# An up projection turned round: activations stationary and a DRAM bounce in place of weights stationary, in a float32 decoder layer

## The chip, the cores and the metric

The kernel runs on one core of a Trainium2 chip. The metric is the device time of one execution in microseconds (us), lower is better. Besides the timed runs there is one execution recorded by the hardware profiler; all rows below come from it. The engines are PE (TensorE, matmul), DVE (VectorE), ACT (ScalarE), POOL (GpSimd) and SP (SyncE, which here issues nearly all DMAs).

## The reference, cut to what matters

One decoder layer on 256 tokens of width 2048: two attention mixers, gates and an output projection, then a squared-ReLU MLP of inner width 8192. The change is in the MLP:

```python
h2 = rms_norm(x, g_mlp)
x = x + jnp.square(jax.nn.relu(h2 @ w_up)) @ w_down      # w_up 2048 x 8192, w_down 8192 x 2048
```

All tensors are float32. The kernel keeps nearly float32 accuracy by splitting each operand into a rounded part *hi* and a rest *lo* and summing three products, hi·hi, hi·lo and lo·hi.

## The kernel before, in words

**Slots.** The whole weight traffic is cut into *slots*. A slot is a weight tile of two 128-row k-blocks by 512 columns. A 1 MB DMA (L127, issued by SP) brings the weights of two slots into a tile `raw` (3 buffers). For each slot `split` makes `hi` on ACT (L138, a cast) and `lo` on DVE (L139, a subtraction); these have 3 buffers each, and a new one can be written once PE has finished with the one three slots back. The main loop is written out by hand: in turn `j` it emits `split(j + 2)`, the DMA of a later piece if one is due, what tables `at_dma[j]` and `at_post[j]` hold, and then the matmuls of slot `j`. So each engine gets its instructions in the order of the turns, and waits in that order.

**Chunks.** Eight slots (k = 2048) make a chunk of 512 output columns. All projections but the up projection go through `tok_chunk`: the activations, transposed and split (`xT`, `yT`, `mT`, `h`, each [128, k-block, hi/lo, 256 tokens]), are the stationary operand, and the split weights the moving one. Two banks of PSUM hold 2 x 128 tokens by 512 columns. Per slot this is `tok_major`: for two token halves and two k-blocks

```python
nc.tensor.matmul(o, lhsT=s_hi, rhs=hi[:, kk, a:b], ...)   # L164
nc.tensor.matmul(o, lhsT=s_hi, rhs=lo[:, kk, a:b], ...)   # L165
nc.tensor.matmul(o, lhsT=s_lo, rhs=hi[:, kk, a:b], ...)   # L166
```

that is 12 matmuls of 512 columns per slot. **The up projection** (`up_chunk`, 8 chunks in each of two halves `hf`) has the operands the other way round: the weights are stationary and `x1T` is moving (L540 hi weight x [hi, lo] tokens, 512 columns; L542 lo weight x hi tokens, 256 columns). Its output comes out feature-major in four PSUM banks, which is the layout that the down projection wants, and `post` (L554 to L563) adds the two halves of a bank, squares the ReLU and splits the result into `h0` or `h1` in three turns after the chunk.

**The bounce.** Where a token-major result must become a stationary operand, `bounce_chunk` turns it. DVE transposes it in 32 x 32 blocks (L198) into `tq`; SP writes `tq` to a DRAM tile `scr` with four DMAs (L203, 128 KB each) and reads it back with one (L208, 512 KB, tile `st`); ACT and DVE then write the hi and lo parts (`split_tr`, L145 and L146, four each). With the chunk's last slot called e, the caller passes j = e + 2, and

```python
on(at_post, j, blk)             # turn e+2: DVE transposes
on(at_dma, j + 1, wr)           # turn e+3: SP writes scr
on(at_dma, j + steps[0], rd)    # steps = (3, 6): turn e+5: SP reads st
on(at_post, j + steps[1], p)    # turn e+8: ACT and DVE unpack
```

`tq` and `st` have one buffer, `scr` two, `tmp` tiles (`u`, `ma`, `mb`) five. The bounce is used before for the queries and keys, for the mixed branches (`mix_b`, default steps) and for the output projection (`out_done`, where the second chunk has steps (5, 9)).

**Order of the stages**: input projection (23 chunks, with attention among the later ones), the branches, the output projection, up and down of half 0, up and down of half 1. The first two chunks of the output projection and of the up projection of half 0 are interleaved by `in_pairs` (first 6 slots of one, 6 of the other, then 2 and 2), since their last k-blocks arrive late. `j_up` is the first slot of the up projection.

Of the kernel before, what the change touches and what calls it, by code (L numbers as in the profile page):

```python
# [9 lines left out]
F32 = mybir.dt.float32  # L10
F32R = mybir.dt.float32r
AF = mybir.ActivationFunctionType
ALU = mybir.AluOpType
AX = mybir.AxisListType

P = 128
S = 256
# [15 lines left out]
CW = 512  # L33
WARM = (10, 7)
EARLY = (1, 2, 3, 4, 5, 6)
KD = D // P
# [30 lines left out]
def hybrid_block_kernel(ctx: ExitStack, tc: tile.TileContext, x, g_mix, w_in, q_norm_a, k_norm_a,  # L67
                        q_norm_b, k_norm_b, rel_bias, w_branch_a, w_branch_b, w_out, g_mlp, w_up,
                        w_down, hot, mask, out):
    nc = tc.nc  # L70
# [13 lines left out]
    def bank(tag="fill"):  # L84
        return ps.tile([P, CW], F32, name=tag, tag=tag)

    def tmp(name="tmp"):
        return tp.tile([P, CW], F32, name=name, tag="tmp")

    at_fill, at_post, at_dma = {}, {}, {}  # L90

    def on(table, j, fn):
        table.setdefault(j, []).append(fn)
# [18 lines left out]
    def stream(src, k0, nk, c0, main, pieces=None):  # L112

        for a in pieces or range(0, nk, 4):
            ap = src[k0 + a * P:k0 + (a + 4) * P, c0:c0 + CW].rearrange("(k p) c -> p k c", p=P)
            for b in (0, 2):
                slots.append((ap, b, a + b, main))
# [24 lines left out]
    def split_tr(dst_hi, dst_lo, src, gain=None):  # L142

        if gain is None:
            nc.scalar.copy(dst_hi, src)  # L145
            nc.vector.tensor_tensor(dst_lo, src, dst_hi.bitcast(F32), op=ALU.subtract)  # L146
        else:
            nc.scalar.activation(dst_hi, src, AF.Copy, scale=gain)
            nc.vector.scalar_tensor_tensor(dst_lo, src, gain, dst_hi.bitcast(F32), op0=ALU.mult,
                                           op1=ALU.subtract)  # L150

    def tok_major(banks, actT, k, first, last, hi, lo, between=None):


        parts = [(0, 0, CW), (1, 0, CW)] if len(banks) == 2 else [(0, 0, CW), (1, 0, S), (1, S, CW)]
        order = [(i, kk) for i in range(len(parts)) for kk in range(2)]
        if between:
            order = [(i, kk) for kk in range(2) for i in range(2)]
        for i, (n, kk) in enumerate(order):
            t, a, b = parts[n]  # L160
            o = banks[n][:, 0:b - a]
            s_hi = actT[:, k + kk, 0, t * P:(t + 1) * P]
            s_lo = actT[:, k + kk, 1, t * P:(t + 1) * P]
            nc.tensor.matmul(o, lhsT=s_hi, rhs=hi[:, kk, a:b], start=first and kk == 0, stop=False)  # L164
            nc.tensor.matmul(o, lhsT=s_hi, rhs=lo[:, kk, a:b], start=False, stop=False)  # L165
            nc.tensor.matmul(o, lhsT=s_lo, rhs=hi[:, kk, a:b], start=False, stop=last and kk == 1)  # L166
            if between and i == 1:
                between()

    def tok_chunk(src, k0, nk, c0, actT, ka, done):  # L170

        st = {}

        def main(j, k, hi, lo):
            if k == 0:
                st["b"] = [bank("acc") for _ in range(2)]
            tok_major(st["b"], actT(), ka + k, k == 0, k + 2 == nk, hi, lo, T.get("mid") if j == 0 else None)
            if k + 2 == nk:
                done(st["b"], j)

        return lambda *p: stream(src, k0, nk, c0, main, p)
# [11 lines left out]
    T = {}  # L193


    def blocks(dst, src):

        nc.vector.transpose(dst.rearrange("p j n r -> p n j r"), src.rearrange("p n (j m) -> p n j m", m=32))  # L198

    def scatter(scr, src):  # L200

        for i in range(4):
            nc.sync.dma_start(out=scr[:, :, :, i].rearrange("t j m f -> m (t j) f"),  # L203
                              in_=src[32 * i:32 * i + 32].rearrange("m t j f -> m (t j) f"))

    def gather(dst, scr):

        nc.sync.dma_start(out=dst, in_=scr.rearrange("t j m i f -> (j m) t (i f)"))  # L208
# [100 lines left out]
    def v_done(br, c):  # L309
        def done(banks, j):  # L310
            def p():
                for t in range(2):
                    o = T["v" + br][:, t, c * CW:(c + 1) * CW]
                    if t:
                        nc.vector.tensor_scalar(o, banks[t], rstd[:, t:t + 1], None, op0=ALU.mult)
                    else:
                        nc.scalar.activation(o, banks[t], AF.Copy, scale=rstd[:, t:t + 1])
            on(at_post, j + 1, p)
        return done
# [141 lines left out]
    def bounce_chunk(src, dst, c, j, gain, steps=(3, 6)):  # L461

        st = {}

        def blk():
            st["tq"] = tq = ap_.tile([P, 2, 4, CW // 4], F32, name="tq")
            for t in range(2):
                blocks(tq[:, t].rearrange("p j (n r) -> p j n r", r=32),
                       src()[t].rearrange("p (n d) -> p n d", d=P))

        def wr():
            st["scr"] = dp.tile([2, 4, 32, 4, CW // 4], F32, name="scr", bufs=2)
            scatter(st["scr"], st["tq"])

        def rd():
            st["st"] = ap_.tile([P, 2, CW], F32, name="st")
            gather(st["st"], st["scr"])

        def p():
            v = st["st"].rearrange("p t (i n r) -> p n t i r", i=4, r=32)  # L480
            for k in range(4):
                hi, lo = (dst()[:, 4 * c + k, a].rearrange("p (t i r) -> p t i r", t=2, i=4) for a in range(2))
                split_tr(hi, lo, v[:, k], None if gain is None else gT[:, gain + 4 * c + k:gain + 4 * c + k + 1])

        on(at_post, j, blk)
        on(at_dma, j + 1, wr)
        on(at_dma, j + steps[0], rd)
        on(at_post, j + steps[1], p)
# [38 lines left out]

    def up_chunk(hf, g):

        st = {}  # L530
        name = f"h{g // 4}"

        def main(j, k, hi, lo):
            if k == 0:
                st["b"] = [bank("fill" if (g + hf) % 2 else "acc") for _ in range(4)]
            for n in range(4):
                b = st["b"][n]
                for kk in range(2):
                    xk = T["x1T"][:, k + kk]
                    nc.tensor.matmul(b, lhsT=hi[:, kk, n * P:(n + 1) * P], rhs=xk.rearrange("p a q -> p (a q)"),  # L540
                                     start=(k + kk == 0), stop=False)
                    nc.tensor.matmul(b[:, S:], lhsT=lo[:, kk, n * P:(n + 1) * P], rhs=xk[:, 0],  # L542
                                     start=False, stop=(k + kk == KD - 1))
            if k + 2 == KD:
                for i in range(3):
                    on(at_post, j + 1 + i, lambda i=i: post(i))

        def post(i):

            if i < 2:  # L550
                for n in (2 * i, 2 * i + 1):
                    u = tmp("u")
                    st[n] = u
                    nc.scalar.copy(u[:, 0:S], st["b"][n][:, S:])  # L554
                for n in (2 * i, 2 * i + 1):
                    u = st[n]
                    nc.vector.tensor_tensor(u[:, S:], st["b"][n][:, 0:S], u[:, 0:S], op=ALU.add)
                    nc.vector.scalar_tensor_tensor(u[:, 0:S], u[:, S:], 0.0, u[:, S:], op0=ALU.max, op1=ALU.mult)
            if i > 0:
                for n in (2 * i - 2, 2 * i - 1):  # L560
                    h = T[name][:, (g % 4) * 4 + n]
                    nc.scalar.copy(h[:, 0], st[n][:, 0:S])
                    nc.vector.tensor_tensor(h[:, 1], st[n][:, 0:S], h[:, 0].bitcast(F32), op=ALU.subtract)  # L563

        return lambda *p: stream(w_up, 0, KD, (hf * 8 + g) * CW, main, p)

    def down_chunk(hf, c):
        st = {}
# [26 lines left out]
    for c in range(23):  # L595
        if c < 6:
            done = qk_done("aq" if c < 3 else "ak", 4 * c)
        elif c < 9:
            done = v_done("a", c - 6)
        elif c < 13:  # L600
            done = qk_done("bq" if c < 11 else "bk", 4 * (c - 9))
        elif c < 15:
            done = v_done("b", c - 13)
        else:
            done = gate_done(c - 15)
# [9 lines left out]
    for hf in range(2):  # L615
        j_half.append(len(slots))
        ups = [up_chunk(hf, g) for g in range(8)]
        if hf:
            for f in ups:
                f()  # L620
        else:
            in_pairs(ups)
        for c in range(4):
            down_chunk(hf, c)
# [8 lines left out]
    for br, nh, tag in (("a", NA, "T0"), ("b", NB, "T2")):  # L633
        t = big.tile([P, 3 * nh * S], F32, name="qkv" + br, tag=tag)
# [57 lines left out]
    for i in range(2, 8):  # L692
        st = {}
# [38 lines left out]
    n = len(slots)  # L732
    done_split, done_load = 2, 3
    for j in range(n + 1):
# [13 lines left out]
        if j < n:  # L748
            hi, lo = split_t.pop(j)
# [38 lines left out]
```

## Time and profile before

| | us |
|---|---|
| median of 3 timed runs | 1409.17 (1408.72 to 1409.3) |
| the profiled execution | 1408.98 |
| its span (first to last instruction) | 1406.9 |
| PE busy | 1401.6 |
| DVE busy | 811.2 |
| ACT busy | 650.2 |
| granted PE clock | 1.00 of full speed (2.4 GHz) throughout |

Busy times are shares of one span and overlap. Matmuls are pipelined, so a busy PE says that matmuls were in flight, not how many columns a second went through; the distance from one matmul's start to the next says that.

### The profile page before, as it was taken

What the parts mean: (1) busy time and instruction counts of PE and PEld (TensorE: products, weight loads), DVE (VectorE), ACT (ScalarE), POOL (GpSimd) and SP (SyncE); (2) the same over time, 40 slices, a digit from 0 to 9 for tenths busy, and PEclk for the clock granted to TensorE, in tenths of its full rate; (3) what the DMA queues carried; (4) which work ended last, traced back from release to release, by engine and by line L of the source; (5) the groups of instructions that cost most, each with busy time, mean ns of one, the idle gap of its engine ahead of it and who ended that gap; (6) DMA issues with size and microseconds to landing.
All of it is one profiled execution on the core that took longest, in us unless ns stands there. A gap on an engine that the chain in (4) does not pass through costs nothing.

```text
span 1406.9 us, 17199 instructions
## 1 busy us (share of the span) xinstructions
PE 1401.6 (100%) x6773; PEld 1179.3 (84%) x6773; DVE 811.2 (58%) x989; ACT 650.2 (46%) x956; POOL 28.6 (2%) x44
## 2 busy tenths in 40 slices
PE   9999999999999999999999999999999999999998
PEld 7888888888888888888888888888888888888888
DVE  5556546676555545766656666444445656554443
ACT  7554445554444464445545445333334444443332
POOL 1101000010000000000000000000000000000000
PEclk9999999999999999999999999999999999999999
DMA  8777986778566655888766655656566566656662
GB/s 284 230 240 230 284 276 220 242 255 279 183 222 210 219 183 181 261 279 276 245 203 192 188 180 182 206 182 203 184 199 190 180 184 188 195 182 215 203 208 91
DMA packets 171128, 300.95 MB, mean 214 GB/s; under 512 B 6936, under 2 KB 37032, under 8 KB 171048
## 3 DMA queue, kind: packets, MB, share of 16 engines
q1 hardware_dynamic: 170856, 299.84, 66.1%
q8 instruction: 53, 0.87, 0.3%
q14 instruction: 27, 0.22, 0.0%
q0 software_dynamic: 160, 0.01, 0.0%
q10 hardware_dynamic: 32, 0.01, 0.0%
HBM read 280.43 MB, written 19.40 MB: 213 GB/s over the span
## 4 chain that ended last, share of the span: by engine, by line
PE 99%; DMA 0%; DVE 0%; issue 0%
PE acc L164 20%; PE acc L165 20%; PE acc L166 20%; PE fill L540 9%; PE acc L540 9%; PE acc L542 4%; PE fill L542 4%; PE fill L164 4%; PE fill L165 4%; PE fill L166 4%; PE fill L383 1%; PE fill L430 1%; PE fill L382 0%; PE fill L432 0%; PE fill L220 0%; DMA x<-in_x_dram 0%
## 5 line engine op out<-in xcount | busy, mean ns | idle before, releaser
L139 DVE TENSOR_TENSOR lo<-raw,hi 128x1024 fp32r<-128x1024 f32 (+1 forms) x498 | 606.3, 1219 | 573.7 <-ACT hi L138 572.3
L138 ACT CAST hi<-raw 128x1024 fp32r<-128x1024 f32 (+1 forms) x498 | 522.3, 1049 | 701.1 <-PE acc L166 422.0
L164 PE MATMUL acc<-hi,xT 128*128 128x512 f32 x736 | 289.4, 393 | 0.0
L165 PE MATMUL acc<-lo,xT 128*128 128x512 f32 x736 | 286.7, 390 | 0.0
L166 PE MATMUL acc<-hi,xT 128*128 128x512 f32 x736 | 286.6, 389 | 0.0
L540 PE MATMUL acc<-x1T,hi 128*128 128x512 f32 x512 | 181.3, 399 | 0.0
L540 PE MATMUL fill<-x1T,hi 128*128 128x512 f32 x512 | 181.3, 399 | 0.0
L166 PEld LDWEIGHTS acc<-hi,xT 128*128 128x128 f32 x736 | 138.2, 188 | 29.0
L164 PEld LDWEIGHTS acc<-hi,xT 128*128 128x128 f32 x736 | 138.4, 188 | 28.8 <-issue 0.6
L165 PEld LDWEIGHTS acc<-lo,xT 128*128 128x128 f32 x736 | 138.3, 188 | 28.6 <-DVE lo L139 0.4
L542 PE MATMUL acc<-x1T,lo 128*128 128x256 f32 x512 | 143.8, 281 | 0.0
L542 PE MATMUL fill<-x1T,lo 128*128 128x256 f32 x512 | 143.8, 281 | 0.0
L540 PEld LDWEIGHTS acc<-x1T,hi 128*128 128x128 f32 x512 | 96.2, 188 | 24.1
L540 PEld LDWEIGHTS fill<-x1T,hi 128*128 128x128 f32 x512 | 96.2, 188 | 24.1
L164 PE MATMUL acc<-hi,h 128*128 128x512 f32 (+1 forms) x288 | 108.7, 377 | 0.0
L166 PE MATMUL acc<-hi,h 128*128 128x512 f32 (+1 forms) x288 | 108.7, 377 | 0.0
L165 PE MATMUL acc<-lo,h 128*128 128x512 f32 (+1 forms) x288 | 108.6, 377 | 0.0
L542 PEld LDWEIGHTS fill<-x1T,lo 128*128 128x128 f32 x512 | 96.7, 189 | 0.0
L542 PEld LDWEIGHTS acc<-x1T,lo 128*128 128x128 f32 x512 | 96.7, 189 | 0.0
L165 PE MATMUL fill<-lo,h 128*128 128x512 f32 (+1 forms) x256 | 96.4, 376 | 0.0
L164 PE MATMUL fill<-hi,h 128*128 128x512 f32 (+1 forms) x256 | 96.3, 376 | 0.0
L166 PE MATMUL fill<-hi,h 128*128 128x512 f32 (+1 forms) x256 | 96.2, 376 | 0.0
(123 smaller groups left out, 1199.9 us busy)
## 6 DMA issues: line engine op xcount, KB each, us to landing
raw<-in_w_in_dram SPq DMA_DIRECT2D x89, 1024.0 KB, 5.7
raw<-in_w_up_dram SPq DMA_DIRECT2D x64, 1024.0 KB, 5.3
raw<-in_w_down_dram SPq DMA_DIRECT2D x64, 1024.0 KB, 5.3
raw<-in_w_out_dram SPq DMA_DIRECT2D x16, 1024.0 KB, 5.4
scr<-tq SPq DMA_DIRECT2D x72, 128.0 KB, 5.5
raw<-in_w_branch_b_dram SPq DMA_DIRECT2D x8, 1024.0 KB, 5.7
st<-scr SPq DMA_DIRECT2D x13, 512.0 KB, 5.6
raw<-in_w_branch_a_dram SPq DMA_DIRECT2D x4, 1024.0 KB, 5.4
```

The lines of the kernel that those rows point to most:

```text
L138: nc.scalar.copy(hi[:, o], t[:, o])
L139: nc.vector.tensor_tensor(lo[:, o], t[:, o], hi[:, o].bitcast(F32), op=ALU.subtract)
L164: nc.tensor.matmul(o, lhsT=s_hi, rhs=hi[:, kk, a:b], start=first and kk == 0, stop=False)
L165: nc.tensor.matmul(o, lhsT=s_hi, rhs=lo[:, kk, a:b], start=False, stop=False)
L166: nc.tensor.matmul(o, lhsT=s_lo, rhs=hi[:, kk, a:b], start=False, stop=last and kk == 1)
L383: nc.tensor.matmul(b[:, P:P + S], lhsT=q[:, 1], rhs=k, start=True, stop=True)
L430: nc.tensor.matmul(st["o"][:, o:o + S], lhsT=v[:, 0, h * HD:(h + 1) * HD], rhs=pt[:, 0:2], start=(g == 0 or not joint), stop=False)
L540: nc.tensor.matmul(b, lhsT=hi[:, kk, n * P:(n + 1) * P], rhs=xk.rearrange("p a q -> p (a q)"), start=(k + kk == 0), stop=False)
L542: nc.tensor.matmul(b[:, S:], lhsT=lo[:, kk, n * P:(n + 1) * P], rhs=xk[:, 0], start=False, stop=(k + kk == KD - 1))
```

## The change

The up projection becomes a `tok_chunk` like the others: `x1T` is stationary, the split weights move, and two banks hold the result token-major. After the chunk ACT takes the ReLU from PSUM into a `tmp` tile, DVE multiplies it with the bank once more (a square of the ReLU), and `bounce_chunk` with the default steps transposes it through DRAM into `h0` or `h1`. The order of chunks, `in_pairs` for half 0 and the down projection stay as they are.

```diff
     def up_chunk(hf, g):
-        def main(j, k, hi, lo):
-            if k == 0:
-                st["b"] = [bank("fill" if (g + hf) % 2 else "acc") for _ in range(4)]
-            for n in range(4):
-                b = st["b"][n]
-                for kk in range(2):
-                    xk = T["x1T"][:, k + kk]
-                    nc.tensor.matmul(b, lhsT=hi[:, kk, n * P:(n + 1) * P], rhs=xk.rearrange("p a q -> p (a q)"),
-                                     start=(k + kk == 0), stop=False)
-                    nc.tensor.matmul(b[:, S:], lhsT=lo[:, kk, n * P:(n + 1) * P], rhs=xk[:, 0],
-                                     start=False, stop=(k + kk == KD - 1))
...
-        def post(i):
...
-        return lambda *p: stream(w_up, 0, KD, (hf * 8 + g) * CW, main, p)
+        def done(banks, j):
+            hs = []
+
+            def p():
+                for t in range(2):
+                    u = tmp("u")
+                    nc.scalar.activation(u, banks[t], AF.Relu)
+                    nc.vector.tensor_tensor(u, banks[t], u, op=ALU.mult)
+                    hs.append(u)
+            on(at_post, j + 1, p)
+            bounce_chunk(lambda: hs, lambda: T[f"h{g // 4}"], g % 4, j + 2, None)
+        return tok_chunk(w_up, 0, KD, (hf * 8 + g) * CW, lambda: T["x1T"], 0, done)
```

In the order of PE's instructions, the first slot of the up projection (slot `j_up`) reads before as follows; `acc_5348` to `acc_5351` are the four banks, `hi_5304` and `lo_5305` the slot's weights, and "..." stands where the second k-block repeats the two rows.

```order
L540 MATMUL acc_5348<-x1T_4690,hi_5304 128x512
L542 MATMUL acc_5348<-x1T_4690,lo_5305 128x256
...
L540 MATMUL acc_5349<-x1T_4690,hi_5304 128x512
L542 MATMUL acc_5349<-x1T_4690,lo_5305 128x256
...
L540 MATMUL acc_5350<-x1T_4690,hi_5304 128x512
L542 MATMUL acc_5350<-x1T_4690,lo_5305 128x256
...
L540 MATMUL acc_5351<-x1T_4690,hi_5304 128x512
L542 MATMUL acc_5351<-x1T_4690,lo_5305 128x256
```

The same slot of the changed kernel, on PE:

```order
L164 MATMUL acc_5348<-hi_5304,x1T_4690 128x512
L165 MATMUL acc_5348<-lo_5305,x1T_4690 128x512
L166 MATMUL acc_5348<-hi_5304,x1T_4690 128x512
...
L164 MATMUL acc_5349<-hi_5304,x1T_4690 128x512
L165 MATMUL acc_5349<-lo_5305,x1T_4690 128x512
L166 MATMUL acc_5349<-hi_5304,x1T_4690 128x512
```

Sixteen matmuls (8 of 512 and 8 of 256 columns) became twelve of 512; the slot streams 6144 columns both times.

SP's queue behind the interleaved pair of half 0 held only weight loads before. In the changed kernel it stands as follows; the pair's first chunk writes `scr_5665` and reads `st_5715`, its second `scr_5717` and `st_5756`.

```order
L203 DMA scr_5665<-tq_5646 32x8x128 x4
L127 DMA raw_5694<-in_w_up_dram 128x4x512
L208 DMA st_5715<-scr_5665 128x2x512
L203 DMA scr_5717<-tq_5696 32x8x128 x4
L127 DMA raw_5738<-in_w_up_dram 128x4x512
L208 DMA st_5756<-scr_5717 128x2x512
L127 DMA raw_5774<-in_w_up_dram 128x4x512
L127 DMA raw_5816<-in_w_up_dram 128x4x512
```

Two bounces of five DMAs each now stand among the weight loads, and the read into `st_5756` stands ahead of the load of `raw_5774`; `st_5715` and `st_5756` are the same single buffer.

ACT's queue at the same place in the changed kernel (turns `j_up + 21` to `j_up + 25`): the casts of weights (`hi`) and the unpacking of the two bounces into `h0`.

```order
L138 CAST hi_5770<-raw_5644 128x1024
L145 CAST h0_5368<-st_5715 128x256 x4
L138 CAST hi_5796<-raw_5694 128x1024
L138 CAST hi_5812<-raw_5694 128x1024
L145 CAST h0_5368<-st_5756 128x256 x4
L138 CAST hi_5838<-raw_5738 128x1024
L536 ACTIVATE u_5842<-acc_5676 128x512
L536 ACTIVATE u_5845<-acc_5677 128x512
L138 CAST hi_5862<-raw_5738 128x1024
```

The unpacking of the second bounce stands two casts behind that of the first, and the casts of the following slots stand behind it.

## Rows read from the trace of the kernel before

**Rows 1.** The page: the span, the busy time of the engines with its share and number of instructions, and the chain of work that ended last by engine.

```profile
span 1406.9 us, 17199 instructions
PE 1401.6 (100%) x6773; PEld 1179.3 (84%) x6773; DVE 811.2 (58%) x989; ACT 650.2 (46%) x956; POOL 28.6 (2%) x44
PE 99%; DMA 0%; DVE 0%; issue 0%
```

**Rows 2.** Busy time by stretch: up of half 0, down of half 0, up of half 1, down of half 1. Columns: stretch, its length, busy time of PE, of the weight loads on PE, of DVE, ACT and POOL (instructions in brackets), granted clock, share of the DMA engines, GB/s.

```profile
691.20:872.10 180.90, 180.90 (x1025) 156.82 (x1024) 113.96 (x163) 88.16 (x132) 0.00 (x0) 1.00 0.62 192
872.10:1046.20 174.10, 174.10 (x770) 144.19 (x769) 86.66 (x82) 69.83 (x72) 0.00 (x0) 1.00 0.59 193
1046.20:1227.10 180.90, 180.90 (x1025) 156.76 (x1025) 109.78 (x150) 83.35 (x120) 0.00 (x0) 1.00 0.60 186
1227.10:1402.90 175.80, 175.80 (x866) 149.11 (x864) 85.42 (x82) 67.69 (x70) 0.00 (x0) 1.00 0.56 183
```

**Rows 3.** PE in order of time (start, duration, instruction) at the end of the output projection and the start of the up projection. Starts are to be compared; the durations overlap.

```profile
690.76 0.39 PE L165 MATMUL acc<-lo,mT 128*128 128x512 f32 x1
690.99 0.39 PE L166 MATMUL acc<-hi,mT 128*128 128x512 f32 x1
691.22 0.39 PE L540 MATMUL acc<-x1T,hi 128*128 128x512 f32 x1
691.44 0.28 PE L542 MATMUL acc<-x1T,lo 128*128 128x256 f32 x1
691.56 0.40 PE L540 MATMUL acc<-x1T,hi 128*128 128x512 f32 x1
691.79 0.28 PE L542 MATMUL acc<-x1T,lo 128*128 128x256 f32 x1
691.91 0.40 PE L540 MATMUL acc<-x1T,hi 128*128 128x512 f32 x1
```

**Rows 4.** Groups of instructions by line and shape over the whole span (count, busy us, mean ns of one, idle time before): the first five are those that the change removes outside PE, the others are operations of the same shape as those it adds.

```profile
L554 ACT COPY u<-acc 128x256 f32<-128x256 f32 x32 | 10.2, 370 | 0.0
L562 ACT CAST h<-u 128x256 fp32r<-128x256 f32 x64 | 23.1, 409 | 1.2 <-DVE u L558 1.2
L557 DVE TENSOR_TENSOR u<-acc,u 128x256 f32<-128x256 f32 x32 | 13.4, 418 | 0.0
L558 DVE SCALAR_TENSOR_TENSOR u<-u 128x256 f32<-128x256 f32 x64 | 27.2, 425 | 2.2
L563 DVE TENSOR_TENSOR h<-u,h 128x256 fp32r<-128x256 f32 x64 | 24.1, 418 | 0.0
L333 ACT ACTIVATE G<-acc,rstd 128x512 f32<-128x512 f32 x6 | 4.1, 679 | 0.0
L497 DVE TENSOR_TENSOR mb<-acc,G 128x512 f32<-128x512 f32 x8 | 5.5, 684 | 0.0
```

**Rows 5.** DVE, ACT and SP in order of time around a bounce of `mix_b` (start, duration of the run, instruction, count, and in brackets the idle time before it and what ended it).

```profile
561.40 1.30 DVE L198 STREAM_TRANSPOSE tq<-ma 128x512 f32<-128x512 f32 x2
562.73 2.06 SPq L203 DMA_DIRECT2D scr<-tq  x4
568.83 0.38 SPq L208 DMA_DIRECT2D st<-scr  x1
574.42 1.05 ACT L138 CAST hi<-raw 128x1024 fp32r<-128x1024 f32 x1 [1.67 <-PE acc L166]
575.38 1.32 ACT L145 CAST mT<-st 128x256 fp32r<-128x256 f32 x4
577.72 1.43 DVE L146 TENSOR_TENSOR mT<-st,mT 128x256 fp32r<-128x256 f32 x4
```

**Rows 6.** An ordinary slot of the output projection, whose first matmul started at 604.14: PE's first matmul, and a cast and a subtraction 13 slots on.

```profile
604.14 0.39 PE L164 MATMUL acc<-hi,mT 128*128 128x512 f32 x1
639.70 1.05 ACT L138 CAST hi<-raw 128x1024 fp32r<-128x1024 f32 x1 [1.67 <-PE acc L166]
640.79 1.23 DVE L139 TENSOR_TENSOR lo<-raw,hi 128x1024 fp32r<-128x1024 f32 x1 [1.50 <-ACT hi L138]
```

**Rows 7.** DMAs by line: size of one and median us from issue to landing; then the least, median and greatest landing time of the reads into `st`.

```profile
raw<-in_w_up_dram SPq DMA_DIRECT2D x64, 1024.0 KB, 5.3
scr<-tq SPq DMA_DIRECT2D x72, 128.0 KB, 5.5
st<-scr SPq DMA_DIRECT2D x13, 512.0 KB, 5.6
DMA to landing us min/median/max: 3.9/5.6/6.9
```

**Rows 8.** Who waited for whom from 520 to 690 us (branches and output projection, with seven bounces), longest first in total: total us, times, longest.

```profile
ACT hi L138 <- PE acc L166: 83.5, 55, 1.7
DVE lo L139 <- ACT hi L138: 59.1, 42, 1.8
ACT junk L514 <- DVE x L512: 6.7, 3, 2.9
DVE tq L198 <- DMA scr<-tq: 0.8, 1, 0.8
ACT hi L138 <- ACT hi L138: 0.5, 2, 0.3
```

**Rows 9.** Busy time by stretch, with the columns of rows 2: a stretch of the input projection, and one that begins 4 us before the output projection and covers its first 36 us.

```profile
160.00:200.00 40.00, 40.00 (x178) 33.11 (x178) 19.69 (x17) 16.22 (x17) 0.00 (x0) 1.00 0.88 283
600.00:640.00 40.00, 40.00 (x178) 33.11 (x178) 24.59 (x30) 17.52 (x23) 0.00 (x0) 1.00 0.86 294
```

More of the change, by code (lines that the diff above doesn't have):

```diff
@@ L528, in up_chunk @@
     def up_chunk(hf, g):
-        st = {}
-        name = f"h{g // 4}"
-        def main(j, k, hi, lo):
-            if k == 0:
-                st["b"] = [bank("fill" if (g + hf) % 2 else "acc") for _ in range(4)]
-            for n in range(4):
-                b = st["b"][n]
-                for kk in range(2):
-                    xk = T["x1T"][:, k + kk]
-                    nc.tensor.matmul(b, lhsT=hi[:, kk, n * P:(n + 1) * P], rhs=xk.rearrange("p a q -> p (a q)"),
-                                     start=(k + kk == 0), stop=False)
-                    nc.tensor.matmul(b[:, S:], lhsT=lo[:, kk, n * P:(n + 1) * P], rhs=xk[:, 0],
-                                     start=False, stop=(k + kk == KD - 1))
-            if k + 2 == KD:
-                for i in range(3):
-                    on(at_post, j + 1 + i, lambda i=i: post(i))
-        def post(i):
-            if i < 2:
-                for n in (2 * i, 2 * i + 1):
-                    u = tmp("u")
[L553 to L563, printed above, removed]
-        return lambda *p: stream(w_up, 0, KD, (hf * 8 + g) * CW, main, p)
+        def done(banks, j):
+            hs = []
+            def p():
+                for t in range(2):
+                    u = tmp("u")
+                    nc.scalar.activation(u, banks[t], AF.Relu)
[4 more added lines that the diff above has]
+        return tok_chunk(w_up, 0, KD, (hf * 8 + g) * CW, lambda: T["x1T"], 0, done)
     def down_chunk(hf, c):
```

## Prediction

> **What bounds the kernel now.** I read the page first: PE is busy for 1401.6 of 1406.9 us, and the chain that ended last is 99% PE [rows 1]. DVE and ACT have 40% and more to spare. So the time is how long PE takes for its matmuls, and a change counts if it alters PE's pace or makes PE wait. Next I asked for busy time by stage, since 100% busy does not say how fast the columns go through. Up and down of a half have 64 slots each, and a slot streams 6144 columns in both (up: 8 x 512 + 8 x 256; down: 12 x 512). Yet up takes 180.9 us and down of half 0 takes 174.1, both with PE busy throughout at full clock [rows 2]. Per slot this is 180.9 / 64 = 2.827 us against 174.1 / 64 = 2.720.
>
> The order of starts shows why. A 512-column matmul followed by another starts its follower 0.227 us later (690.76, 690.99, 691.22); a pair of up (512 + 256 columns) takes 691.56 - 691.22 = 0.34 to 0.35 us, and 2.827 / 8 = 0.353 on the mean [rows 3]. If one column went through in each cycle of 2.4 GHz, 512 columns would take 0.213 us and 768 would take 0.320: about 0.013 us are lost on each matmul of the token-major kind and 0.033 on a pair. The up projection has 1024 x 2 = 2048 matmuls for columns that fit in 1536.
>
> **The change on PE.** Per slot, 16 matmuls become 12, of the same shape, operand layout and order as in all other projections. I price them at the pace of down of half 0, the nearest stage with as many slots: 174.1 us for 64. Two halves: 2 x (180.9 - 174.1) = **13.6 us saved**. The bounds are close: the output projection's 0.227 us gives 12 x 0.227 x 64 = 174.3 per half, so 13.2 saved.
>
> One rule speaks against it. The Trainium skill (TensorE: Matmul & The Clock Gate, "Back-to-back issue gap") gives a warm matmul of N columns a gap of N / 2.4 + 2.5 ns. By that, up would now take 8 x (215.8 + 109.2) = 2600 ns a slot and the change 12 x 215.8 = 2590, which saves 1.3 us in all. The measured gaps of 0.227 and 0.353 us lie well above the rule's, and by unequal amounts, so the trace does not bear it out.
>
> **ACT and DVE.** Removed per chunk: on ACT 4 x 0.370 + 4 x 0.409 = 3.1 us, on DVE 4 x (0.418 + 0.425 + 0.418) = 5.0 [rows 4]. Added: on ACT two ReLUs from PSUM at 0.68 (the nearest row is L333) and four unpacking casts in 1.32, 2.7 in all; on DVE two products at 0.684, two transposes in 1.30 and four subtractions in 1.43, 4.1 in all [rows 4, 5]. Both engines have less to do, so no gain or loss on the path. What matters is lumps in a single slot. In an ordinary slot the cast starts 0.2 us after PE starts the slot (639.70 against 604.14 + 13 x 2.72 = 639.50) and the subtraction ends at +2.5; PE needs the pair only two slots after, at +5.44 [rows 6]. So a split is 2.9 us early. The lumps (1.28, 1.30 and 1.43 on DVE behind 1.23 of subtraction) fit in a slot of 2.72 each, hidden by that lead.
>
> **The bounce, an ordinary chunk.** Let e be the chunk's last slot. The products end at e+2 plus 1.1 us, the transposes at e+3 plus 1.1 (subtraction to +2.5, then 1.30). SP's writes go out then; in the mix stage SP's read follows the writes by 568.83 - 562.73 = 6.1 us, and lands 5.6 later [rows 5, 7]. So `st` is there 11.7 us on, at e+7 plus 1.9. The unpacking comes up on ACT at e+8 plus 1.25: 2.1 us early, 0.8 with the longest landing of 6.9. SP's own waits cost nothing: the loads behind them leave at the end of their slot's split as before, and nothing on SP is behind a wait longer than that. The last chunk's `h1` is unpacked by e+9 plus 1.2, and down reads those k-blocks first in slot e+15. So 0 for 15 of 16 bounces. The precedent is the same bounce with the same distances among the same kind of slots: from 520 to 690 us there were seven, and no wait there is of a weight cast or of PE for one; the one DMA wait is 0.8 us on DVE [rows 8].
>
> **The bounce of the interleaved pair.** This one has no precedent. In half 0, chunk a ends at slot 13 and b at 15, and both use the one buffer `st` with the default distances. The read for b (turn 20) cannot start until ACT and DVE have unpacked a, which they do in turn 21: cast to +1.25, subtraction to +2.5, then four L146 in 1.43, so done at slot 22 plus 1.2. The read lands 5.6 later, at slot 24 plus 1.4. ACT reaches b's unpacking at slot 23 plus 1.25, so **it waits 2.9 us**, and behind it stand the casts of slots 26 and on, for which PE waits. Unpacking 1.32, cast 1.0, subtraction 1.2: the weights of slot 26 are ready at slot 25 plus 2.2, 0.5 us before PE wants them. With the longest landing of 6.9 they come 0.8 late. Bounds 0 and 0.8; the median row gives 0, but transfers pile up there, so I take **0.3**. SP's load behind that read (`raw_5774`) leaves at slot 22 plus 1.6 instead of 21 plus 2.5, 1.8 later, and is wanted by the cast in turn 26, 9 us on, against 5.3 of landing [rows 7].
>
> **The sum** against the profiled execution's own 1408.98: 1408.98 - 13.6 + 0.3 = 1395.7. The median of the runs is 0.2 above it, so **1395.8 us**, 0.95% faster. What this measurement can tell from no change is about 0.2%, 2.8 us.
>
> **Rivals.**
>
> *The bounce is late now and then (1397 to 1406).* Weights and five more DMAs a chunk share SP's queue. If the bounce takes longer than 11.7 us, ACT holds back the casts. PE waits once the unpacking starts later than e+9 plus 1.9 (1.32 + 1.0 + 1.2 before slot e+11), that is from 17.1 us of bounce on. For: two landings in a row, and the pair's margin of 0.5 us. Against: the waits of [rows 8], and a spare of 5.4 us. If half of the chunks lost 0.5 us: 1395.8 + 4 = 1400.
>
> *The DMA engines become the bound (slower).* A chunk brings 4.2 MB of weights, and now also 0.52 written and 0.52 read, 5.24 MB in 8 x 2.72 = 21.76 us: 241 GB/s where the up stage now moves 186 to 192 [rows 2]. If only 220 were to be had with 512-byte pieces among them, a chunk would take 23.8 us, 2.0 more, and 16 of them 33: 1429. It decides at the 22.6 us that a chunk takes now, 232 GB/s. Against it: 283 and 294 GB/s were moved with PE busy for all of 40 us [rows 9].
>
> *PE does not get faster (no change).* If a matmul cost what the cited rule says, or if the slower pace of up came from `x1T` and not from the number of matmuls, the gain would be 1.3 us or 0: 1407.7 to 1409. Against: `h` and `mT` as stationary tiles run at that pace [rows 2, 3].
>
> **How the numbers follow.** Forecast as worked out, 1394.6 to 1397: 0.75. Late bounces: 0.16, of which all but 0.02 stay more than 0.2% faster. DMA bound: 0.05, slower but for 0.01. No faster PE: 0.04, of which 0.03 lies within 0.2% and 0.01 slower. So faster 0.89, same 0.06, slower 0.05. The range goes from 1394.6 (13.6 saved, no wait, and 0.6 for the scatter of runs and a slightly quicker pace) to 1400, which takes in most of the late bounces.
>
> **What would show it.** PE's starts in up at 0.227 us and up stages of 174 us each, with no PE idle time in either. ACT's L145 waiting for the `st` read at the pair, 23 x 2.72 + 1.3 = 64 us after the start of up, for about 3 us, and at no other chunk. DMA at about 240 GB/s in the up stages. It is wrong if PE's starts there are 0.235 us apart, or if casts wait for `raw` or for L145 in each chunk.

## The result, and the profile after

The changed kernel takes 1394.92 us (median of 5 runs, 1394.75 to 1395.86) against 1409.17 before: a ratio of 0.9901, with a 95% interval of 0.9886 to 0.9915. The profiled execution took 1394.88, 14.1 us less than the 1408.98 of the one before. The forecast was 1395.8, with a range from 1394.6 to 1400.

The page of the changed kernel, against [rows 1]: span, busy times, the chain by engine.

```profile
span 1392.8 us, 16170 instructions
PE 1387.0 (100%) x6261; PEld 1153.0 (83%) x6261; DVE 802.7 (58%) x925; ACT 649.1 (47%) x924; POOL 28.6 (2%) x44
PE 99%; DVE 0%; POOL 0%; ACT 0%; issue 0%; POOLq 0%
```

PE has 512 instructions less and is still the bound, busy all the time. Busy time by stretch of the changed kernel, against [rows 2]: up of half 0, down of half 0, up of half 1, down of half 1, with the same columns.

```profile
691.00:865.10 174.10, 174.10 (x770) 144.21 (x769) 109.05 (x133) 87.39 (x118) 0.00 (x0) 1.00 0.77 242
865.10:1039.10 174.00, 174.00 (x769) 144.15 (x768) 87.20 (x82) 69.73 (x70) 0.00 (x0) 1.00 0.61 200
1039.10:1213.20 174.10, 174.10 (x769) 144.19 (x768) 104.88 (x119) 82.93 (x106) 0.00 (x0) 1.00 0.77 236
1213.20:1388.90 175.70, 175.70 (x865) 149.09 (x863) 86.03 (x82) 67.59 (x68) 0.00 (x0) 1.00 0.58 189
```

Both up stages went from 180.9 to 174.1 us, the pace of the down stage; 2 x 6.8 = 13.6 us. The bounce shows in the last column only: 242 and 236 GB/s where 192 and 186 stood. PE's starts at the same place, against [rows 3]:

```profile
690.75 0.39 PE L166 MATMUL acc<-hi,mT 128*128 128x512 f32 x1
690.97 0.39 PE L164 MATMUL acc<-hi,x1T 128*128 128x512 f32 x1
691.20 0.39 PE L165 MATMUL acc<-lo,x1T 128*128 128x512 f32 x1
691.43 0.39 PE L166 MATMUL acc<-hi,x1T 128*128 128x512 f32 x1
```

The step from start to start is 0.227 us, the same before and after the border between the projections. The up projection starts at 690.97 instead of 691.22: 0.25 us of the 14.1 arose in code that is the same in both kernels. The remaining 0.25 is spread over the down stages and the tail, 0.1 or less in each.

The waits of the changed kernel from 691 to 1213 us (both up stages and the first down stage):

```profile
ACT hi L138 <- PE acc L166: 280.6, 188, 1.7
DVE lo L139 <- ACT hi L138: 218.9, 186, 1.8
DVE tq L198 <- DMA scr<-tq: 2.0, 1, 2.0
ACT junk L514 <- DVE x L512: 1.9, 1, 1.9
ACT h L145 <- DMA st<-scr: 0.8, 1, 0.8
```

ACT's casts wait for PE (a buffer that PE still reads), and no row has PE waiting. The sixteen bounces made two waits in all, 2.0 us on DVE and 0.8 on ACT, both at the interleaved pair.

### The profile page after: what moved, and what is told of

Its sections match the earlier page's. It is cut to its first block, busy times and chain, and to the rows that moved or that the text cites. A ratio compares the mean times of both kernels' runs of the same rounds, so it can differ in the third digit from the quotient of the medians.

```text
span 1392.8 us, 16170 instructions
## 1 busy us (share of the span) xinstructions
PE 1387.0 (100%) x6261; PEld 1153.0 (83%) x6261; DVE 802.7 (58%) x925; ACT 649.1 (47%) x924; POOL 28.6 (2%) x44
## 4 chain that ended last, share of the span: by engine, by line
PE 99%; DVE 0%; POOL 0%; ACT 0%; issue 0%; POOLq 0%
PE acc L165 28%; PE acc L164 28%; PE acc L166 28%; PE fill L165 4%; PE fill L166 4%; PE fill L164 4%; PE fill L383 1%; PE fill L430 1%; PE fill L382 0%; PE fill L432 0%; PE fill L220 0%; PE acc L650 0%; DVE xT L149 0%; PE fill L351 0%; DVE lo L139 0%; DVE x L563 0%
## 5 line engine op out<-in xcount | busy, mean ns | idle before, releaser
L164 PE MATMUL acc<-hi,x1T 128*128 128x512 f32 x512 | 199.2, 389 | 0.0
L165 PE MATMUL acc<-lo,x1T 128*128 128x512 f32 x512 | 199.2, 389 | 0.0
L166 PE MATMUL acc<-hi,x1T 128*128 128x512 f32 x512 | 199.2, 389 | 0.0
L166 PEld LDWEIGHTS acc<-hi,x1T 128*128 128x128 f32 x512 | 96.1, 188 | 20.0
L164 PEld LDWEIGHTS acc<-hi,x1T 128*128 128x128 f32 x512 | 96.1, 188 | 19.9
L165 PEld LDWEIGHTS acc<-lo,x1T 128*128 128x128 f32 x512 | 96.1, 188 | 19.9
L166 PEld LDWEIGHTS acc<-hi,h 128*128 128x128 f32 x288 | 54.2, 188 | 10.0
L165 PEld LDWEIGHTS acc<-lo,h 128*128 128x128 f32 x288 | 54.2, 188 | 9.9
```

## Experiments: what sets PE's pace

**The same columns in narrower matmuls.** The question was whether the number of matmuls sets the pace, or which operand is stationary.

```diff
+    def tok_narrow(banks, actT, k, first, last, hi, lo):
+        for t in range(2):
+            for a in (0, S):
+                for kk in range(2):
+                    o = banks[t][:, a:a + S]
...
+                    nc.tensor.matmul(o, lhsT=s_hi, rhs=lo[:, kk, a:a + S], start=False, stop=False)
...
+            if src is w_up:
+                tok_narrow(st["b"], actT(), ka + k, k == 0, k + 2 == nk, hi, lo)
```

> The changed kernel with the up projection's matmuls cut into 256 columns: 24 of them a slot in place of 12 of 512, same stationary tiles, same columns, same bounce. Theory (every matmul loses a fixed piece, so their number counts): 256-column matmuls start 0.118 us apart, as in the last chunk of the kernel before, so a slot takes 24 x 0.118 = 2.83 us, an up stage of 64 slots 181.3, and the whole about 1394.9 + 2 x (181.3 - 174.1) = 1409: the gain is gone. Rival (the slower pace came from having the weights stationary, not from the number): 2.72 us a slot and 1395.

Measured: 1416.08 us (1415.85 to 1416.65), ratio to before 1.0049 (1.0034 to 1.0064). PE in the up stage of this kernel, start by start, and then the first up stage's row of busy times:

```profile
800.90 0.28 PE L162 MATMUL acc<-hi,x1T 128*128 128x256 f32 x1
801.02 0.28 PE L159 MATMUL acc<-hi,x1T 128*128 128x256 f32 x1
801.14 0.28 PE L161 MATMUL acc<-lo,x1T 128*128 128x256 f32 x1
```

```profile
692.00:876.30 184.30, 184.30 (x1538) 184.30 (x1537) 109.32 (x133) 87.06 (x118) 0.00 (x0) 1.00 0.76 229
```

The step is 0.120 us, not 0.118, so a slot takes 24 x 0.120 = 2.88 and the stage 184.3; the whole gain is gone and more. If one column goes through in each cycle of 2.4 GHz, a 256-column matmul in a run of its kind is 0.120 - 256 / 2400 = 0.0133 us over its columns, and a 512-column one is 0.2267 - 512 / 2400 = 0.0133 over its own: the same loss for each matmul at both widths. The rival's 1395 is out. Each matmul here has a weight load of its own (1538 and 1537 in the row), so the runs do not tell a loss per matmul from one per load; in this kernel the loads are busy for all of the 184.30 us.

**Weights stationary, all matmuls wide.** The kernel before, with the lo weights multiplied with all 512 columns.

```diff
-                    nc.tensor.matmul(b[:, S:], lhsT=lo[:, kk, n * P:(n + 1) * P], rhs=xk[:, 0],
+                    nc.tensor.matmul(b, lhsT=lo[:, kk, n * P:(n + 1) * P], rhs=xk.rearrange("p a q -> p (a q)"),
```

> The kernel before with the lo weights multiplied with all 512 columns (a fourth product, lo x lo, is added: 2048 more columns a slot). Weights stay stationary, the matmuls of a slot are 16 of 512. If the pace depends on the matmul's width alone: 0.2267 us from start to start, 3.63 us a slot, 232.1 an up stage, 1409 + 2 x (232.1 - 180.9) = 1511. If stationary weights cost more (the 0.233 us from a 512 to the next start in the kernel before): 3.73 a slot, 238.9 a stage, 1525.

Measured: 1511.74 us (one run). PE in its up stage, and the first up stage's row:

```profile
800.91 0.39 PE L540 MATMUL fill<-x1T,hi 128*128 128x512 f32 x1
801.14 0.39 PE L542 MATMUL fill<-x1T,lo 128*128 128x512 f32 x1
801.36 0.39 PE L540 MATMUL fill<-x1T,hi 128*128 128x512 f32 x1
```

```profile
691.70:923.80 232.10, 232.10 (x1026) 192.19 (x1025) 114.65 (x163) 88.04 (x133) 0.00 (x0) 1.00 0.48 150
```

The step is 0.227 us with the weights stationary too, and the stage is 232.1 as worked out. So which operand is stationary does not set the step.

**Weights stationary, the widths grouped.** With 0.2267 and 0.120 the old slot should take 8 x 0.3467 = 2.773 us and its stage 177.5; it took 180.9. What had not been tried was the order, and the missing 3.4 us a stage were looked for there.

```diff
             for n in range(4):
                 b = st["b"][n]
                 for kk in range(2):
                     xk = T["x1T"][:, k + kk]
                     nc.tensor.matmul(b, lhsT=hi[:, kk, n * P:(n + 1) * P], rhs=xk.rearrange("p a q -> p (a q)"),
                                      start=(k + kk == 0), stop=False)
+            for n in range(4):
+                b = st["b"][n]
+                for kk in range(2):
+                    xk = T["x1T"][:, k + kk]
                     nc.tensor.matmul(b[:, S:], lhsT=lo[:, kk, n * P:(n + 1) * P], rhs=xk[:, 0],
                                      start=False, stop=(k + kk == KD - 1))
```

> The kernel before with the order of its up matmuls changed alone: in each slot first the eight of 512 columns, then the eight of 256, no more alternation; weights stay stationary, no bounce. If a matmul of 512 costs 0.2267 us and one of 256 costs 0.118 wherever they stand, the slot takes 8 x 0.345 = 2.76 us, an up stage 176.5 and the whole 1409.2 - 8.8 = 1400.4. If the loss sits in having weights stationary or in the number alone, with nothing lost by alternating, 1409 as before.

Measured: 1405.07 us (1404.74 to 1405.47), ratio 0.997 (0.9959 to 0.9981), 4.3 us faster than before and 4.7 short of the forecast. PE in order of time, runs of one line merged (L546 is the matmul of lo, L542 before):

```profile
800.06 2.00 PE L540 MATMUL acc<-x1T,hi 128*128 128x512 f32 x8
801.90 1.11 PE L546 MATMUL acc<-x1T,lo 128*128 128x256 f32 x8
802.86 2.00 PE L540 MATMUL fill<-x1T,hi 128*128 128x512 f32 x8
```

The eight narrow ones take 802.86 - 801.90 = 0.96, 0.120 each; the eight wide ones 1.84, which is 0.027 more than 8 x 0.2267. So the wide ones lose something behind narrow ones, and more so when they alternate one by one.

**Two by two, and the same mix with the activations stationary.** Two runs were made to see how that extra goes with the order, and whether the operand has a part in it. The first edits the kernel before; for each bank it has two wide matmuls, then two narrow ones.

```diff
                     nc.tensor.matmul(b, lhsT=hi[:, kk, n * P:(n + 1) * P], rhs=xk.rearrange("p a q -> p (a q)"),
                                      start=(k + kk == 0), stop=False)
+                for kk in range(2):
+                    xk = T["x1T"][:, k + kk]
                     nc.tensor.matmul(b[:, S:], lhsT=lo[:, kk, n * P:(n + 1) * P], rhs=xk[:, 0],
```

The second edits the changed kernel: in the up projection the function below takes the place of `tok_major`, and its third product is two narrow matmuls.

```diff
+    def tok_narrow(banks, actT, k, first, last, hi, lo):
...
+                nc.tensor.matmul(o, lhsT=s_hi, rhs=hi[:, kk], start=first and kk == 0, stop=False)
+                nc.tensor.matmul(o, lhsT=s_hi, rhs=lo[:, kk], start=False, stop=False)
+                for a in (0, S):
+                    nc.tensor.matmul(o[:, a:a + S], lhsT=s_lo, rhs=hi[:, kk, a:a + S], start=False,
+                                     stop=last and kk == 1 and a == S)
```

> The kernel before with its up matmuls in the order wide, wide, narrow, narrow for each bank (512, 512, 256, 256), weights stationary. With eight wide and eight narrow grouped, the wide ones took 1.84 us a slot, 0.027 more than 8 x 0.2267, and alternating one by one cost 0.053 more. If each narrow matmul leaves a debt that half a wide one repays (four slow wide ones after eight narrow ones), two by two costs 0.027 a slot as well: 2.80 a slot, 1405. If every return from narrow to wide slows up to four wide ones, all eight are slow: 2.827 a slot and 1409 as before.

> The changed kernel with the same mix of widths as the kernel before: the third product of each group (lo activations) is cut into two of 256 columns, so that a slot has eight matmuls of 512 and eight of 256 in the order wide, wide, narrow, narrow, with the activations stationary and the bounce in place. If only number and order of the widths count, this takes per slot what the two-by-two kernel takes with the weights stationary, 2.80 us by the first theory: 1395 + 128 x 0.08 = 1405; or 2.827 by the second: 1409. If stationary activations are faster for themselves: below 1400.

Measured: 1403.98 us (1403.82 to 1404.33), ratio 0.9964 (0.995 to 0.9978), for the first, 1403.97 (1403.61 to 1404.36), ratio 0.9963 (0.9948 to 0.9978), for the second. The first matmuls on `x1T` and on `h` of each, from their rows by tile (least, median and greatest duration in ns, first and last start in us); the first pair is of the kernel with the weights stationary:

```profile
L540 PE MATMUL acc<-x1T,hi x512: 389/396/398, 691.4 to 1221.7; 128*128 128x512 f32 x171
L164 PE MATMUL acc<-hi,h x288: 283/389/395, 869.8 to 1397.5; 128*128 128x512 f32 x128, 128*128 128x256 f32 x16
```

```profile
L158 PE MATMUL acc<-hi,x1T x512: 389/396/396, 691.1 to 1221.1; 128*128 128x512 f32 x171
L176 PE MATMUL acc<-hi,h x288: 283/389/395, 869.4 to 1397.1; 128*128 128x512 f32 x128, 128*128 128x256 f32 x16
```

The up stages are 869.8 - 691.4 = 178.4 and 869.4 - 691.1 = 178.3 us: with the same mix in the same order it makes no difference which operand is stationary, or whether there is a bounce. Over the 177.5 of the fixed loss they are 0.9 and 0.8, where one by one is 3.4. Neither theory on the size of this extra held (2.80 or 2.827 a slot; it was 2.79). PE's starts in the two-by-two kernel, with the weights stationary, show why:

```profile
800.10 0.63 PE L540 MATMUL acc<-x1T,hi 128*128 128x512 f32 x2
800.56 0.40 PE L544 MATMUL acc<-x1T,lo 128*128 128x256 f32 x2
800.79 0.63 PE L540 MATMUL acc<-x1T,hi 128*128 128x512 f32 x2
801.26 0.39 PE L544 MATMUL acc<-x1T,lo 128*128 128x256 f32 x2
```

Two wide ones take 0.46 to 0.47 us, where two in a run of their kind take 2 x 0.2267 = 0.453; two narrow ones take 0.23, where two in a run of theirs take 0.24. So every return to wide is slow, as the second theory had it, but the narrow ones are quicker, which neither theory had, and the 0.9 is the difference of the two. What causes either stays open.

## Experiments: what the bounce costs

**Without the trip through DRAM.**

```diff
-            st["tq"] = tq = ap_.tile([P, 2, 4, CW // 4], F32, name="tq")
+            st["tq"] = tq = ap_.tile([P, 2, 4, CW // 4], F32, name="tq", tag="tq" if trip else ("sa", "ts")[c % 2])
...
-            v = st["st"].rearrange("p t (i n r) -> p n t i r", i=4, r=32)
+            v = (st["st"] if trip else st["tq"].rearrange("p t j f -> p t (j f)")).rearrange(
+                "p t (i n r) -> p n t i r", i=4, r=32)
...
-        on(at_dma, j + 1, wr)
-        on(at_dma, j + steps[0], rd)
+        if trip:
+            on(at_dma, j + 1, wr)
+            on(at_dma, j + steps[0], rd)
```

`trip` is false in the up projection. The transposed tile is held until the unpacking there, and so it alternates between two buffers instead of using one.

> The changed kernel without the trip through DRAM in the up projection: the five DMAs of each of 16 bounces are left out and the unpacking reads the 32 x 32 transposed tile directly (so the tokens and features of h are permuted; the transposes, the unpacking and all matmuls stay). If the bounce is hidden: the same time as the changed kernel, 1394.9 within 0.5, DMA traffic of the up stages back to about 195 GB/s. If the bounce costs anything on the path, this is faster by that: 0.05 us a chunk would be 0.8.

Measured: 1395.74 us (1395.42 to 1396.07), ratio 0.9903 (0.9887 to 0.992), not faster than the changed kernel, and 0.3 us outside the forecast. Its first up stage:

```profile
692.10:866.20 174.10, 174.10 (x769) 144.15 (x769) 109.14 (x132) 87.41 (x118) 0.00 (x0) 1.00 0.63 200
```

The up projection began at 692.1 instead of 691.0 us, in code before the edit, and the stage took 174.1 like that of the changed kernel, with DMA at 200 GB/s in place of 242. The trip costs nothing on the path.

**The pair's second bounce later.**

```diff
-            bounce_chunk(lambda: hs, lambda: T[f"h{g // 4}"], g % 4, j + 2, None)
+            bounce_chunk(lambda: hs, lambda: T[f"h{g // 4}"], g % 4, j + 2, None,
+                         (5, 9) if hf == 0 and g == 1 else (3, 6))
```

> The changed kernel with the interleaved pair's second bounce at steps (5, 9), as the output projection has them, in place of (3, 6): its unpacking then comes three turns later. ACT's one wait of 0.8 us for the read of st goes away. Since the weights of the slot behind it were 2.6 us early even so, the time stays at 1394.9 within 0.5. If that wait did reach PE, up to 0.8 faster.

Measured: 1395.38 us (1395.2 to 1395.49), ratio 0.99 (0.9885 to 0.9915). ACT's wait for the read of `st` is gone from the list (of the waits for bounces between 691 and 1213 us only one of 2.1 us on DVE is left), and the time did not fall: the wait never reached PE.

**Two bounces, and three.**

```diff
             scatter(st["scr"], st["tq"])
+            for i in range(more):
+                st[i] = dp.tile([2, 4, 32, 4, CW // 4], F32, name=f"scx{i}", bufs=2)
+                scatter(st[i], st["tq"])
...
             gather(st["st"], st["scr"])
+            for i in range(more):
+                x = ap_.tile([P, 2, CW], F32, name=f"sx{i}", tag=("sa", "ts")[i])
+                gather(x, st[i])
```

`more` is 1 in the up projection of one kernel and 2 in that of the other.

> The changed kernel with each bounce of the up projection done twice: four more writes of 128 KB to a second DRAM tile and one more read of 512 KB into a tile that nothing uses. A chunk then moves 6.29 MB in 21.76 us, 289 GB/s. Theory (traffic of this size hides behind PE, since 294 GB/s went by with PE busy before): 1395 within 1. Rival (the DMA engines are near their bound at 241 GB/s): slower by 8 us and more, each us of a chunk counting 16 times.

> As the kernel with two bounces, with a third: 7.34 MB a chunk, 337 GB/s to keep PE's pace, more than any stretch of the kernel before shows (294). If 294 is about the ceiling, a chunk takes 25.0 us, 3.2 more, and 16 of them 51: 1446. If the queue has room up to 337: still 1395.

Measured: two bounces 1396.26 us (1396.05 to 1396.4), ratio 0.9906 (0.9891 to 0.9921); three 1419.34 (1418.67 to 1422.02), ratio 1.0068 (1.0052 to 1.0085). With two bounces, the first up stage, two stretches of 20 us in it, and the second up stage:

```profile
691.50:866.60 175.10, 174.36 (x769) 143.98 (x768) 108.52 (x132) 87.08 (x118) 0.00 (x0) 1.00 0.88 281
740.00:760.00 20.00, 19.26 (x85) 15.65 (x84) 9.93 (x13) 7.78 (x11) 0.00 (x0) 1.00 1.05 328
800.00:820.00 20.00, 20.00 (x90) 16.57 (x89) 13.28 (x16) 9.58 (x13) 0.00 (x0) 1.00 0.97 311
1040.60:1214.80 174.20, 174.20 (x771) 144.23 (x770) 104.87 (x119) 83.15 (x106) 0.00 (x0) 1.00 0.87 277
```

Both up stages with three:

```profile
691.40:879.80 188.40, 179.29 (x770) 145.75 (x769) 107.76 (x131) 85.22 (x114) 0.00 (x0) 0.98 0.91 288
1053.00:1238.40 185.40, 179.56 (x782) 146.24 (x782) 104.87 (x120) 81.47 (x103) 0.00 (x0) 1.00 0.91 290
```

Waits of the kernel with three bounces from 691 to 880 us:

```profile
ACT h L145 <- DMA st<-scr: 25.3, 5, 8.1
PEld acc L165 <- DVE lo L139: 6.6, 5, 2.4
ACT hi L138 <- DMA raw<-in_w_up_dram: 6.5, 5, 1.3
PE acc L165 <- DVE lo L139: 4.7, 5, 2.0
PE acc L164 <- ACT hi L138: 4.4, 3, 3.4
```

Two bounces end 1.3 us over the changed kernel, a little more than the 1 that was left open. Of this, 0.5 us arose before the up projection, which began at 691.5; the first up stage is 1.0 us longer and the second, at 277 GB/s, only 0.1. The 281 GB/s are a mean over a stage whose first 40 us hold no bounce of the up projection. PE stood around the interleaved pair (19.26 us busy of 20, at 328 GB/s), and at 311 GB/s in a later stretch it was busy throughout. So it was the pair that paid for the second bounce.

With three bounces the stages are 14 and 11 us longer. The means of 288 and 290 are no ceiling either: from 740 us on, stretches of 20 us moved 296 to 328 GB/s in the first stage, but 337 were wanted. The time lies between the two forecasts, 24 us over the changed kernel. The way in which it is lost is the one that the prediction described for late bounces: ACT stands at the unpacking (up to 8.1 us, at the pair's second bounce) and the casts of the next slots stand behind it. Late weight loads are there as well, 6.5 us on ACT.

## Why the prediction was right, point by point

**The gain on PE** was sized as it came: 13.6 us from the pace of the down stage, 13.6 measured. That price came from a row of the same kernel with the same shape of matmul. **The reason given for it was half of it.** The prediction put the gain down to 2048 matmuls for columns that fit in 1536. The fixed loss of 0.0133 us, shown by the narrow and the all-wide kernels, makes 512 x 0.0133 = 6.8 us of that. The other 6.8 lay in alternating wide and narrow ones. They could have been told apart beforehand: [rows 3] has 0.12 us from a narrow start to the next wide one, which leaves 0.353 - 0.12 = 0.233 for the wide matmul, against 0.227 among wide ones. I took the pair's mean and did not split it. The total came out because the price was taken from a stage with the same matmuls, whatever the reason for its pace.

The profiled time was 0.8 us below the sum's 1395.7. Of this, 0.3 is the term for the interleaved pair (below), and 0.5 arose in code that is the same in both kernels; that the measured time lies close to the lower end of the range is owed to these and not to the change.

**The rule of the Trainium skill** (TensorE: Matmul & The Clock Gate, "Back-to-back issue gap") gives N / 2.4 + 2.5 ns, and calls this the gap of an isolated matmul and not that of a stream of weight loads and matmuls. The estimate by it was 1408.98 - 1.3 = 1407.7. No kernel run here agrees: the loss is 13.3 ns a matmul at both widths, where the page has 2.5.

**ACT and DVE** were to have less to do, DVE by 16 x 0.9 = 14 us and ACT by 16 x 0.4 = 6 over the span: DVE's busy time fell by 8.5 us and ACT's by 1.1. The saving was priced too high, in part because the removed operations were taken at the mean duration of one, although their records overlap in a run ([rows 4]: 64 casts at 0.409 us would be 26.2, their busy time is 23.1). This is off the path: no cast was late for PE.

**The ordinary bounce** cost nothing, as forecast, and its times came out close. SP's read follows the writes by 6.5 to 6.9 us (6.1 assumed), as in the third and fourth chunk of half 0:

```profile
762.73 3.58 SPq L203 DMA_DIRECT2D scr<-tq  x4
769.67 0.38 SPq L208 DMA_DIRECT2D st<-scr  x1
...
784.49 2.51 SPq L203 DMA_DIRECT2D scr<-tq  x4
790.95 0.38 SPq L208 DMA_DIRECT2D st<-scr  x1
```

**The interleaved pair** was the one term of the sum that was mis-sized: +0.3 us in the sum, 0 measured. The place and the mechanism were right. SP, ACT and DVE at the pair's second bounce:

```profile
751.97 0.38 SPq L208 DMA_DIRECT2D st<-scr  x1
755.55 1.33 ACT L145 CAST h<-st 128x256 fp32r<-128x256 f32 x4 [0.76 <-DMA st<-scr]
756.78 1.05 ACT L138 CAST hi<-raw 128x1024 fp32r<-128x1024 f32 x1
757.86 1.22 DVE L139 TENSOR_TENSOR lo<-raw,hi 128x1024 fp32r<-128x1024 f32 x1 [0.45 <-ACT hi L138]
```

The read went out at slot 22 plus 1.2 (690.97 + 22 x 2.72 + 1.2 = 752.0), as worked out, and ACT stood for it at the foreseen place, 64 us into the stage. But the data were there 3.6 us later, not 5.6, so ACT waited 0.76 us and not 2.9. The weights of slot 26 were ready at 759.1, 2.6 us before PE came to them at 761.7. The median landing of all such reads was too dear for this one: in the changed kernel they landed after 3.6 to 7.1 us, 5.3 in the median, so this was the quickest, and the 0 is in part luck. By the same working a landing of 7.1 would have made the weights 0.9 us late. The wait of 2.0 us on DVE, for the single buffer `tq` while the first bounce was still being written, was not in the prediction; the lead of the splits hid it.

**The rivals.** No DMA bound showed at 220 GB/s: 242 were needed and cost nothing, stretches of 311 went by beside a busy PE, and it is the 337 of three bounces that could not be had. That PE would get no faster is excluded by the up stages of 174.1 us; that its pace hangs on which operand is stationary, by the all-wide and the mixed kernels. With one bounce the only late one was the pair's second, by 0.8 us on ACT and nothing on PE.

## What to carry to other kernels

Where PE is the bound, price a rearranged matmul by the step between starts in a stage of the same shape, not by its columns: here a matmul in a run of one width cost its columns plus 13.3 ns, and mixed widths cost something more, so of the orders tried 512 columns throughout was the cheapest for the same columns, and which operand was stationary made no difference. A layout change could then go through DRAM, since the result was due a good while after the transfer. A mean DMA rate over a stage does not say how near it was to its limit: with two bounces the time was lost in one stretch, where the transfers of two chunks piled up. A buffer that two interleaved chunks share is worth a drawing of turns: it shows where an engine will stand in its queue, even where the lead of the work behind hides it.

## What was not expected of the hardware

Mixed widths cost more than the steps of uniform runs add up to: with eight matmuls of 512 and eight of 256 columns a slot, alternating took 3.4 us a stage over the fixed loss, eight and eight 1.2 (up stage 178.7), two by two 0.9. In the last of these the wide ones were slower than in a run of their kind and the narrow ones quicker. The two-by-two order, which changes nothing but the order of the instructions, made the kernel before 5.0 us faster. The cause was not found.

With three bounces the granted clock of the first up stage was 0.98; the other stages shown here have 1.00. PE in it, at the pair's second bounce:

```profile
764.10 0.39 PE L166 MATMUL acc<-hi,x1T 128*128 128x512 f32 x1
767.87 0.80 PE L164 MATMUL acc<-hi,x1T 128*128 128x512 f32 x1 [3.38 <-ACT hi L138]
...
771.00 0.63 PE L166 MATMUL acc<-hi,x1T 128*128 128x512 f32 x1
771.43 0.63 PE L164 MATMUL acc<-hi,x1T 128*128 128x512 f32 x1
```

PE had stood for 3.38 us, and behind this wait its starts are 0.43 us apart, which is 512 columns at 1.2 GHz, where they were 0.227 apart before.
